# Four sets of seven products for the eight gate blocks of a hybrid decoder layer

## The chip, the cores and the metric

The kernel runs on one core of one Trainium2 chip. A core has TensorE (PE, matrix products; PEld is its weight load), VectorE (DVE), ScalarE (ACT), GpSimd (POOL) and SyncE (SP, which here only issues transfers), an on-chip memory of 128 partitions (SBUF), accumulation banks for TensorE (PSUM) and DMA engines that move data between HBM and SBUF. The engines run side by side and meet at semaphores. The metric is the time of one execution on the device in microseconds; a median of several runs is compared.

## The reference, cut to what matters

A layer for 256 tokens of width 2048. The input is normalised and projected by `w_in`; latent attention (`attn`) and a gated short convolution run beside each other; each result is projected to the width of the model, weighted by a gate from the same input, and the sum is projected once more.

```python
h = _rmsnorm(x, pre_norm_g)
proj = jnp.einsum('bsd,de->bse', h, w_in)
... z_mla, c_in, b_gate, c_gate, z_conv, g_mla, g_conv = jnp.split(proj, cuts, axis=-1)
...
y_mla = jnp.einsum('bse,ed->bsd', attn, w_o_mla)
y_conv = jnp.einsum('bse,ed->bsd', b_gate * conv * jax.nn.silu(z_conv), w_o_conv)
merged = jax.nn.sigmoid(g_mla) * y_mla + jax.nn.sigmoid(g_conv) * y_conv
out = jnp.einsum('bsd,de->bse', merged, w_out)
x = x + _rmsnorm(out, post_norm_g)
```

The change concerns `g_mla`, `g_conv`, `y_mla`, `y_conv` and `merged`: five products of 256x2048 by 2048x2048, the last with `w_out`.

## The kernel before

**Numbers.** Everything is float32, computed by three products of a high and a low part: each weight `raw` is split into `whi` (ScalarE, line 254) and `wlo` (VectorE, line 255), in halves of 128x1024. One weight load ("unit") is 1 MB, four rows of 128 by a column block of 512.

**Blocks.** Each of the five matrices has four column blocks of 512. A plain block is four units of 24 products of 128x512, so 96 products. For the gates there is a cheaper way, `paired` (line 1188): two blocks are taken as a 2x2 problem, the input halves in seven prepared combinations (`form` "11", "5", "6", "7", "22", "3", "12"), the weights in four plain and three summed ones, and seven products take the place of eight. A set has seven items, Q1, V5, V6, V7, V4, V3, Q2, each of two units of 12 products: 168 products for two blocks. The sums are made in SBUF buffers `b` of 8 KB a partition (tags `rt`, `rb`, `rc`, two each): VectorE adds at V5, V6 and V4 (line 1204), and an accumulating DMA of GpSimd adds at V5 what V7 uses (line 1208). V4 loads the `rb` buffers a second time.

**Which blocks.** `paired(c)` takes column c of both gates, c = 1, 2, 3. Column 0 is plain (`gate_block`, line 1109).

**Stages.** A loop over 16 heads (line 902) computes attention and convolution; it keeps x in `x_both`. The forms are made in its first half, stored in HBM (`far_form`) and fetched by `bring_form` (line 1037). Behind the loop the pools of the loop are closed and new ones are laid over them on the right side: `wides` (gates and products, 2 KB each), `sraw` (the sums' buffers) and `forms` (seven times 8 KB). `seq` is a list of units, each with a load, a split, its products and something to do after; the loop at line 1376 issues loads up to four loads ahead and splits two units ahead. Its order: gate block 0 of `g_mla`, of `g_conv`, set 1 with the branch blocks p0 and p1 between its items, set 2 with p2 and most of p3, set 3 with the rest of p3, v0 and v1, then v2 and v3. Here p is `y_mla`, v is `y_conv`, and `at_u`/`cv_u` fetch a quarter of their inputs, turned, into `at_both`/`cv_both`, which take the place of `x_both`. Then comes the output product in the order of `out_order`, and the tail with the last norm and the stores.

**Gates.** A finished gate is written to HBM (`keep`, line 1024) and read again (`again`, line 1030) when its branch block is done: `branch_block` multiplies p by its gate and keeps the product `m`; `merged_block` reads gate and `m`, multiplies and adds, turns the sum and stores it to `far_m` for the output product.

**Queues.** Loads of weights, forms and quarters go out on SP's queue in the order of the program; each waits on SP until its buffer is free. The buffers `raw` (three) are shared by plain units and quarters. Accumulating loads, `m` and `far_m` go out on GpSimd's queue, kept gates on ScalarE's. While the loop runs, `ahead` (line 209) loads three units and splits one unit ahead of the products, past the end of the loop too.

**PSUM.** Plain blocks use four banks `mm`; a set has X (tag `cv`, two), Z (`st`) and Y (`o`).

Of the kernel before, what the change touches and what calls it, by code (L numbers as in the profile page):

```python
# [11 lines left out]
F32 = mybir.dt.float32  # L12
# [70 lines left out]
def tile_layer(ctx: ExitStack, tc: tile.TileContext, xw, w0, xb, x, pos, pvec, post_g, wc, wz, wcv, wkr, wqk, wqr, wv, cwr, wsq, xf, out):  # L83
# [65 lines left out]
    done = {"raw": 0, "split": 0}  # L149

    def load_raw(i):
# [11 lines left out]
        for a, b, piece in pieces:  # L163
            d = nc.sync.dma_start(out=t[:, a:b], in_=piece)
            if i >= u_d[0][0][0]:
                tc.keep_in_program_order(d)
# [6 lines left out]
    def split_unit(i):  # L173
# [22 lines left out]
        for h in range(0, w, HALF):  # L196
            n = min(HALF, w - h)
            if u_out[3, 0] <= i < u_out[3, 3]:
                both = sraw.tile([P, 2, HALF], F32R, name=f"whl{i}_{h}", tag=SRAW[len(last_parts) % 3], bufs=2)
# [9 lines left out]
    def ahead(i, raw=3, split=1):  # L209
        while done["raw"] < min(i + raw, len(plan)):  # L210
            load_raw(done["raw"])
            done["raw"] += 1
        while done["split"] < min(i + 1 + split, len(plan)):
# [79 lines left out]
    xstack = main.enter_context(ExitStack())  # L293
    hp = xstack.enter_context(tc.tile_pool(name="hp", bufs=1))
    x_both = hp.tile([P, KD, 2 * S], F32R, name="x_both")
# [8 lines left out]
    qa = bp.tile([P, KR, 2 * S], F32R, name="qa")  # L304
    ckv = bp.tile([P, KR, 2 * S], F32R, name="ckv")
# [106 lines left out]


# [472 lines left out]

    form_steps = make_forms()
# [14 lines left out]
    for h in range(H):  # L902
        v, at = divmod(h, HV)

        if at == 0:
# [57 lines left out]
        if h < 8:  # L963
            next(form_steps)
            next(form_steps)

# [40 lines left out]
    estack.close()  # L1007
    right = ctx.enter_context(ExitStack())
    wides = right.enter_context(tc.tile_pool(name="wides", bufs=1, side="right", reuse_waits="tile"))
    sraw = right.enter_context(tc.tile_pool(name="sraw", bufs=1, side="right", reuse_waits="tile"))  # L1010
    gstack = ExitStack()
    forms = gstack.enter_context(tc.tile_pool(name="forms", bufs=1, side="right", reuse_waits="tile"))
    SRAW = ("rt", "rb", "rc")
    last_parts = []

    def sum_tile(name, tag):
        return sraw.tile([P, UNIT], F32, name=name, tag=tag, bufs=2)
# [15 lines left out]


    form = {n: forms.tile([P, KH, 2, P], F32R, name=f"form_{n}") for n in FORMS}

    def bring_form(n):
        tc.keep_in_program_order(
            nc.sync.dma_start(
                out=form[n][:, :, :, :].rearrange("p k j c -> p (k j c)").bitcast(F32), in_=far_form[n][:, :]  # L1040
            )
        )
# [66 lines left out]
    def gate_block(c, n, key, afters):  # L1109

        def last(pss):
            for t in range(NT):
                g = wide(f"sg{n}_{c}_{t}", "abcd"[2 * n + t])
                nc.scalar.activation(g[:, :], pss[t][:, :], AF.Sigmoid, scale=r_col[:, t : t + 1])
                keep((key, c, t), g)
            if 3 in afters:
                afters[3]()

        return block(c, n, lambda k: x_both[:, k, :], afters, last)

    def branch_block(c, both):

        y = []

        def early():
            for t in range(NT):
                y.append(wide(f"y{c}_{t}", "y", 2))
                again(("gm", c, t), y[t])

        def last(pss):  # L1130
            if c == 3:
                for t in range(NT):
                    y.append(wide(f"y{c}_{t}", "y", 2))
                    nc.scalar.activation(y[t][:, :], pss[t][:, :], AF.Copy)
                    keep(("y", c, t), y[t])
                return
            early()
            for t in range(NT):
                nc.vector.tensor_tensor(y[t][:, :], pss[t][:, :], y[t][:, :], op=ALU.mult)
                keep(("m", c, t), y[t])  # L1140

        return block(c, 2, lambda k: both[k // 4][:, k % 4, :], {}, last)

    fetches = []

    def merged_block(c, both):

        got = []

        def fetch(t):  # L1150
            g, m = (
                wide(f"v{n}{c}_{t}", "y", 2) if c < 2 else late.tile([P, 512], F32, name=f"v{n}{c}_{t}")
                for n in "gm"
            )
            again(("gc", c, t), g)
            again(("y" if c == 3 else "m", c, t), m)
            q = None
            if c == 3:
                q = late.tile([P, 512], F32, name=f"vq{t}")
                again(("gm", c, t), q)  # L1160
            got.append((g, m, q))

        def soon():
            if c < 2:
                fetch(0)
            elif c == 2:
                for f in fetches[2:]:
                    for t in range(NT):
                        f(t)

        fetches.append(fetch)

        def last(pss):
            for t in range(NT):
                if len(got) <= t:
                    fetch(t)
                g, m, q = got[t]
                if q:
                    nc.vector.tensor_tensor(m[:, :], m[:, :], q[:, :], op=ALU.mult)
# [426 lines left out]
```

## Time and profile before

| | us |
|---|---|
| median of 3 runs | 1052.83 (1050.6 to 1053.73) |
| the profiled execution, its own time | 1049.99 |
| its span, first to last instruction | 1048.2 |
| TensorE busy | 1022.9 |
| VectorE busy | 784.4 |
| ScalarE busy | 580.0 |
| GpSimd busy | 200.3 |

The core's mean granted TensorE clock was 0.99. Lines of the profile name engine, line, operation and the tiles written and read; a table of stretches gives the busy time of each engine with its number of instructions, the granted clock as a share of full speed, the share of time in which the DMA engines were busy, and GB/s. The chain that ended last is followed back from the last instruction, each step to what released it. A wait is put down to the event that came last. Products overlap by their pipeline, so the time of one is read from a run of them, not from its own duration.

### The profile page before, as it was taken

To read this page: it belongs to the slowest core of one execution; us is meant where nothing else is said; L and a number is where in the kernel's file an instruction comes from. 1 tells how busy PE (TensorE), PEld (TensorE's weight loads), DVE (VectorE), ACT (ScalarE), POOL (GpSimd) and SP (SyncE) were. 2 spreads that over 40 slices of the span, in tenths; PEclk is the share of its full clock that TensorE was granted. 3 is DMA by queue.
4 is the path that set the end of the run, shared out by engine and by line. 5 is a ranking of instruction groups with operands and counts; after the bars stand their busy time and mean duration, and the time that the engine had idled before them with its cause. 6 is when DMAs were issued, how large, how long until landed. Compare 5 with 4: busy or idle time off the path is not lost.

```text
span 1048.2 us, 12876 instructions
## 1 busy us (share of the span) xinstructions
PE 1022.9 (98%) x4576; PEld 845.2 (81%) x4576; DVE 784.4 (75%) x1074; ACT 580.0 (55%) x811; POOL 200.3 (19%) x366
## 2 busy tenths in 40 slices
PE   9999999999999999999999999799999999998997
PEld 8888888878788788888888888678888878887886
DVE  7588978779676687777777756778987968666562
ACT  7675646646555555564555545546666655533551
POOL 4620421112411223212233110000100102142000
PEclk9999999999999999999999999899999999999999
DMA  9776778667777676867676799878786785697742
GB/s 355 280 250 227 272 239 284 237 222 285 261 272 256 231 249 223 269 213 231 245 256 210 271 366 359 271 312 327 236 302 247 272 298 181 241 333 306 290 164 81
DMA packets 55153, 273.13 MB, mean 261 GB/s; under 512 B 9232, under 2 KB 11920, under 8 KB 30512
## 3 DMA queue, kind: packets, MB, share of 16 engines
q1 hardware_dynamic: 35280, 213.30, 55.5%
q0 software_dynamic: 16784, 50.98, 15.6%
q10 hardware_dynamic: 3024, 8.01, 1.9%
q8 instruction: 36, 0.59, 0.2%
q14 instruction: 29, 0.24, 0.1%
HBM read 239.78 MB, written 28.31 MB: 256 GB/s over the span
## 4 chain that ended last, share of the span: by engine, by line
PE 72%; DMA 13%; DVE 9%; issue 4%; ACT 2%; POOL 1%; SPq 0%; DVEq 0%; POOLq 0%; ACTq 0%
PE cv L88 28%; PE sq L88 15%; PE out L88 8%; PE z L88 4%; DMA raw<-wsq_dram 3%; DMA b<-wsq_dram 3%; PE qa L88 2%; DMA far_form<-form 2%; PE sX L88 2%; DVE wlo L255 2%; PE ckv L88 2%; PE kn L88 2%; PE qn L88 2%; DVE slo_V L255 1%; DMA cw<-cwr_dram 1%
## 5 line engine op out<-in xcount | busy, mean ns | idle before, releaser
L255 DVE TENSOR_TENSOR wlo<-raw,whi 128x1024 fp32r<-128x1024 f32 (+1 forms) x316 | 371.8, 1192 | 134.8 <-ACT whi L254 128.6
L254 ACT ACTIVATE whi<-raw 128x1024 fp32r<-128x1024 f32 (+1 forms) x318 | 324.1, 1032 | 267.3 <-PE cv L88 98.4
L88 PE MATMUL cv<-whi,x_both 128*128 128x512 f32 x1024 | 321.0, 390 | 3.1 <-DVE vv_lo L255 3.1
L88 PEld LDWEIGHTS cv<-whi,x_both 128*128 128x128 f32 x1024 | 193.0, 188 | 43.7 <-DVE vv_lo L255 3.9
L88 PE MATMUL cv<-wlo,x_both 128*128 128x512 f32 x512 | 200.1, 391 | 0.8 <-DVE wlo L255 0.8
L88 PEld LDWEIGHTS cv<-wlo,x_both 128*128 128x128 f32 x512 | 96.4, 188 | 21.0 <-DVE wlo L255 1.6
L254 ACT ACTIVATE shi_V<-b 128x1024 fp32r<-128x1024 f32 x60 | 61.9, 1057 | 59.7 <-PE sq L88 26.0
L88 PE MATMUL sq<-whi,at_both 128*128 128x512 f32 x256 | 83.3, 398 | 4.4 <-ACT whi L254 4.4
L255 DVE TENSOR_TENSOR slo_V<-b,shi_V 128x1024 fp32r<-128x1024 f32 x60 | 71.2, 1222 | 19.4 <-ACT shi_V L254 19.0
L88 PE MATMUL z<-whi,x_both 128*128 128x512 f32 x256 | 80.0, 389 | 0.0
L88 PE MATMUL sq<-whi,cv_both 128*128 128x512 f32 x256 | 79.8, 389 | 0.0
L340 POOL DMA_DIRECT2D far<-via x64 | 35.4, 559 | 181.1 <-DVE via L332 178.0
L88 PE MATMUL out<-whi,m_both 128*128 128x512 f32 x208 | 65.6, 395 | 0.0
L88 PEld LDWEIGHTS sq<-whi,at_both 128*128 128x128 f32 x256 | 49.5, 193 | 15.4 <-ACT whi L254 5.1
L88 PEld LDWEIGHTS sq<-whi,cv_both 128*128 128x128 f32 x256 | 48.1, 188 | 10.1 <-ACT shi_V L254 0.2
L88 PEld LDWEIGHTS z<-whi,x_both 128*128 128x128 f32 x256 | 48.1, 188 | 9.9
L88 PE MATMUL sq<-wlo,at_both 128*128 128x512 f32 x128 | 51.6, 403 | 2.1 <-DVE wlo L255 2.1
L88 PE MATMUL z<-wlo,x_both 128*128 128x512 f32 x128 | 49.8, 389 | 0.0
L88 PE MATMUL sq<-wlo,cv_both 128*128 128x512 f32 x128 | 49.8, 389 | 0.0
L88 PE MATMUL sX<-shi_V,form 128*128 128x512 f32 x144 | 47.2, 398 | 1.1 <-ACT shi_V L254 1.1
L88 PEld LDWEIGHTS out<-whi,m_both 128*128 128x128 f32 x208 | 39.8, 191 | 8.4
L88 PE MATMUL out<-wlo,m_both 128*128 128x512 f32 x104 | 41.2, 397 | 3.1 <-DVE wlo L255 3.1
(281 smaller groups left out, 1580.0 us busy)
## 6 DMA issues: line engine op xcount, KB each, us to landing
raw<-wcv_dram SPq DMA_DIRECT2D x64, 1024.0 KB, 5.8
raw<-wsq_dram SPq DMA_DIRECT2D x56, 1024.0 KB, 6.6
b<-wsq_dram SPq DMA_DIRECT2D x24, 1024.0 KB, 7.2
raw<-wz_dram SPq DMA_DIRECT2D x16, 1024.0 KB, 5.1
raw<-wqk_dram SPq DMA_DIRECT2D x8, 1024.0 KB, 6.4
far_form<-form POOLq DMA_DIRECT2D x14, 512.0 KB, 7.9
form<-far_form SPq DMA_DIRECT2D x7, 1024.0 KB, 11.6
cw<-cwr_dram POOLq DMA_DIRECT2D x24, 256.0 KB, 6.4
```

Source lines behind the costliest of these rows:

```text
L88: return tc.keep_in_program_order(nc.tensor.matmul(*a, **kw))
L254: a = nc.scalar.activation(hi, src, AF.Copy)
L255: b = nc.vector.tensor_tensor(lo, src, hi.bitcast(F32), op=ALU.subtract)
L340: tc.keep_in_program_order(queue.dma_start(out=f[i], in_=m))
```

## The change

Eight gate blocks become four sets. A set now takes two column blocks of one gate: `g_mla` columns 0 and 1, 2 and 3, then the same of `g_conv`. The plain gate blocks go, and with them `gate_block` and `merged_block`.

A gate stays in its SBUF tile (`gate_of`) and the sums of a branch block stay in their PSUM banks (`sums_of`); whichever comes second calls `weigh` (the product goes to HBM as `m`) or `merge` (the `m` of the same column is fetched ahead through two tiles `y`, added, turned and stored to `far_m`).

`x_both` becomes four tiles, so that quarters of `at` and `cv` replace it one by one. The latents `qa` and `ckv` get a pool of their own (`lp`), which closes at head 14; over it and the early pool a left pool `fleft` holds forms "11", "5" and the sum buffer `rt0`, and the two forms are fetched at heads 14 and 15. Small tiles of the loop are placed first in their pool so that the other sum buffers and forms, now in one pool `spool` in an order written out by hand, lie over tiles that are released early. The merged quarters lie in `spool` over forms 7, 22, 3 and 12.

The loop's `ahead` stops at the loop's last unit. X moves to bank `st`, Z to `cv`. The order of units within the sets is new, and so is the start of `out_order`.

```diff
-    for n, c in [(0, 0), (1, 0)] + [(n, c) for n in (2, 3) for c in range(4)]:
+    for n, c in [(n, c) for n in (2, 3) for c in range(4)]:
...
-    out_order = [(c, k) for c in range(2) for k in range(3)] + [(0, 3), (1, 3)]
+    out_order = [(0, 0), (0, 1), (1, 0), (1, 1), (0, 2), (1, 2), (0, 3), (1, 3)]
...
-        while done["raw"] < min(i + raw, len(plan)):
+        while done["raw"] < min(i + raw, done["end"]):
...
+        if h == H - 2:
+            estack.close()
+            lstack.close()
+            fleft = main.enter_context(tc.tile_pool(name="fleft", bufs=1, reuse_waits="tile"))
+            for n in ("11", "5"):
+                form[n] = fleft.tile([P, KH, 2, P], F32R, name=f"form_{n}", tag=f"f{n}", bufs=1)
...
+        if h >= H - 2:
+            bring_form(("11", "5")[h - (H - 2)])
...
+    sums = {tag: sum_tile(f"first_{tag}", tag) for tag in ("rt0", "rt1", "rb0", "rb1")}
+    for n in ("3", "12"):
+        form[n] = form_tile(spool, n)
+    sums.update({tag: sum_tile(f"first_{tag}", tag) for tag in ("rc0", "rc1")})
+    for n in ("6", "7", "22"):
+        form[n] = form_tile(spool, n)
...
+    def meet(c, t, combine):
+        met[c, t] = met.get((c, t), 0) + 1
+        if met[c, t] == 2:
+            combine(c, t)
...
+    def weigh(nc_, t):
+        n, c = nc_
+        g = gate_of[n, c, t]
+        nc.vector.tensor_tensor(g[:, :], sums_of[n, c][t][:, :], g[:, :], op=ALU.mult)
+        keep(("m", c, t), g)
...
+    def merge(nc_, t):
+        n, c = nc_
+        g, m = gate_of[n, c, t], fetched.pop((c, t))
+        nc.vector.tensor_tensor(g[:, :], sums_of[n, c][t][:, :], g[:, :], op=ALU.mult)
+        nc.vector.tensor_tensor(m[:, :], m[:, :], g[:, :], op=ALU.add)
+        go, _ = turned(m[:, :], g[:, :], 4, far_m[c][:, 512 * t : 512 * (t + 1)])
+        go()
+        fetch()
...
-            tag, bufs = {"X": ("cv", 2), "Z": ("st", 1), "Y": ("o", 1)}[b]
+            tag, bufs = {"X": ("st", 1), "Z": ("cv", 2), "Y": ("o", 1)}[b]
...
+    s0, s1, s2, s3 = (paired(i, *a) for i, a in enumerate(((0, 0, weigh), (0, 2, weigh), (1, 0, merge), (1, 2, merge))))
...
+    interleave(s0, {
+        "Q1": at_u[:1] + p[0][:1] + at_u[1:2] + p[0][1:2] + at_u[2:3] + p[0][2:3], "V5": at_u[3:] + p[0][3:],
+        "V6": p[1][:1], "V7": p[1][1:2], "V4": p[1][2:3], "Q2": p[1][3:],
     })
+    interleave(s1, {"Q1": p[2][:2], "V5": p[2][2:3], "V6": p[2][3:], "V7": p[3][:2], "V3": p[3][2:3], "Q2": p[3][3:]})
     interleave(s2, {
+        "Q1": cv_u[:1] + v[0][:1] + cv_u[1:2] + v[0][1:2], "V5": cv_u[2:3] + v[0][2:3], "V6": cv_u[3:] + v[0][3:],
+        "V7": v[1][:2], "V3": v[1][2:3], "Q2": v[1][3:],
     })
...
     interleave(s3, {
+        "Q1": v[2][:2], "V5": v[2][2:3], "V6": v[2][3:], "V7": v[3][:1], "V3": v[3][1:2],
     })
```

More of the change, by code (lines that the diff above doesn't have):

```diff
@@ L148, in tile_layer @@
     raws, splits, early = {}, {}, {}
-    done = {"raw": 0, "split": 0}
+    done = {"raw": 0, "split": 0, "end": u_d[0][2][0]}
     def load_raw(i):
@@ L1121, in branch_block @@
[L1121 to L1179, printed above, removed]
-                nc.vector.tensor_tensor(g[:, :], pss[t][:, :], g[:, :], op=ALU.mult)
-                nc.vector.tensor_tensor(m[:, :], m[:, :], g[:, :], op=ALU.add)
-                go, _ = turned(m[:, :], g[:, :], 4, far_m[c][:, 512 * t : 512 * (t + 1)])
-                go()
-        return block(c, 3, lambda k: both[k // 4][:, k % 4, :], {1: soon}, last)
@@ L1271, in paired @@
         out = {}
-        for name, (n, k), _, p, f, b, first, last, after in items:
+        for name, (nb, k), _, p, f, b, first, last, after in items:
             us = []
@@ L1374, in tile_layer @@
+    done["end"] = len(plan)
     nl = ns = 0
@@ L1402, in tile_layer @@
     assert not pending
+    assert not wanted and not fetched
     last_m = turned_unit(far_m[3:4], m_b, 3, nc.gpsimd)
```

205 lines of the change are left out of this document (99 added, 106 removed).

## The prediction

> **What bounds the kernel now.** I read the page's first part, then the chain that ended last, then the waits of PE, and last a table of stretches cut where the program's stages end.
>
> ```profile
> span 1048.2 us, 12876 instructions
> PE 1022.9 (98%) x4576; PEld 845.2 (81%) x4576; DVE 784.4 (75%) x1074; ACT 580.0 (55%) x811; POOL 200.3 (19%) x366
> ```
> ```profile
> 599.00 43.58 PE sq L88 x192
> ...
> 713.53 5.44 PE sZ L88 x24
> ...
> 951.18 88.77 PE out L88 x383
> ```
>
> PE is busy for 98% of the span, so its work is the bound; a stage is longer than its matmuls only where PE waits or its clock drops. The price of a matmul is in the chain (start, duration, engine, tile, count): 192 products of the two plain gate blocks took 43.58 us, and 24 of a set of seven 5.44 us. Both give 0.227 us for one of 128x512 (5.44/24 = 0.2267, used below).
>
> The next rows are the stages: the plain gate blocks, the sets for columns 1, 2 and 3 with what runs between, the last two branch blocks, the output product, the tail (busy times of PE, PEld, DVE, ACT, POOL, then granted clock, DMA share, GB/s).
>
> ```profile
> 598.80:642.90 44.10, 44.10 (x197) 36.50 (x196) 24.92 (x27) 19.78 (x22) 4.94 (x9) 1.00 0.94 368
> 642.90:735.30 92.40, 85.80 (x360) 68.97 (x359) 74.49 (x65) 53.48 (x60) 4.05 (x6) 0.96 0.83 302
> 735.30:811.80 76.50, 76.24 (x336) 62.79 (x336) 66.31 (x56) 49.97 (x53) 4.05 (x6) 1.00 0.73 258
> 811.80:904.30 92.50, 90.11 (x387) 73.08 (x386) 77.31 (x73) 55.49 (x61) 12.39 (x21) 0.98 0.75 261
> 904.30:947.80 43.50, 43.50 (x193) 35.87 (x192) 26.07 (x30) 16.41 (x17) 16.66 (x31) 1.00 0.72 260
> 947.80:1040.00 92.20, 89.06 (x387) 73.34 (x386) 50.26 (x54) 38.22 (x51) 4.79 (x9) 0.98 0.59 222
> 1040.00:1048.20 8.20, 1.92 (x8) 1.04 (x6) 3.06 (x6) 2.12 (x6) 0.00 (x0) 0.78 0.35 129
> ```
>
> From the loops in the code these stages hold 360 products (set 1), 336 (set 2), 384 (set 3), 192 and 384 (output). At 0.2267 us that is 81.6, 76.2, 87.1, 43.5 and 87.1 us. The losses are therefore 92.4 - 81.6 = **10.8**, 0.3, 92.5 - 87.1 = **5.4**, 0 and 92.2 - 87.1 = **5.1**: 21.6 us after 599 us. Part is PE waiting, part a low clock after it:
>
> ```profile
> PE sq L88 <- ACT whi L254: 4.4, 1, 4.4
> PE out L88 <- DVE wlo L255: 3.1, 1, 3.1
> ...
> PE sX L88 <- ACT shi_V L254: 1.1, 1, 1.1
> ```
> ```profile
> 681.00:682.00 1.00, 1.00 (x4) 0.50 0.78 197
> ...
> 683.00:684.00 1.00, 1.00 (x6) 1.00 0.99 410
> ...
> 850.00:852.00 2.00, 2.00 (x5) 0.50 0.46 178
> ...
> 952.00:954.00 2.00, 2.00 (x7) 0.60 0.75 164
> ```
>
> In each loss PE stands still (92.40 - 85.80 = 6.6 us in the first, 2.4 and 3.1 in the others), and then runs at clock 0.50 to 0.60 for some microseconds. So a wait costs nearly twice itself (10.8 to 6.6, 5.4 to 2.4). The Trainium skill, TensorE: Matmul & The Clock Gate, "Part 1: The HAM clock gate", says that only an idle window of about 3.4 us puts the clock at half. By that rule the waits of set 3, the longest of which is 1.1 us, would have cost their own 2.4 us and the forecast would be some 2 us lower; the 0.50 at 850 us speaks against it, and the measurement decides.
>
> **What set 1 lost, and why.** SP issues loads in program order, and a load waits for its buffer, with all behind it:
>
> ```profile
> 577.14 22.64 SPq L164 DMA_DIRECT2D raw<-wsq_dram  x5
> ...
> 645.16 0.33 SPq L164 DMA_DIRECT2D raw<-wsq_dram  x1
> ...
> 657.67 0.33 SPq L164 DMA_DIRECT2D raw<-wsq_dram  x1
> ```
> ```profile
> 657.67 16.56 DMA raw<-wsq_dram
> ```
> ```profile
> 630.00:640.00 10.00, 10.00 (x46) 8.29 (x45) 4.90 (x4) 4.37 (x5) 0.00 (x0) 1.00 1.02 428
> ...
> 650.00:660.00 10.00, 10.00 (x46) 8.26 (x45) 10.00 (x10) 4.96 (x6) 1.99 (x3) 1.00 1.01 292
> ...
> 590.00:600.00 10.00, 10.00 (x49) 8.34 (x48) 8.89 (x12) 7.38 (x10) 0.55 (x1) 1.00 0.58 213
> ```
>
> The load of 657.67 landed 16.56 us later, because the DMA engines were full (share 1.01) with a burst that had waited behind the shared raw buffers. PE's 4.4 us wait is that.
>
> **The change, part by part.**
>
> *Fewer products.* A set of seven needs 7 x 24 = 168 products where two plain blocks need 192. Column 0 was plain; now four sets cover all eight gate blocks: 24 products go, 24 x 0.2267 = **-5.44 us**. PE is the bound and nothing replaces them, so this is on the path.
>
> *More VectorE and ScalarE work.*
>
> ```profile
> L255 DVE TENSOR_TENSOR slo_V<-b,shi_V 128x1024 fp32r<-128x1024 f32 x60 | 71.2, 1222 | 19.4 <-ACT shi_V L254 19.0
> L1204 DVE TENSOR_TENSOR b<-b,b 128x2048 f32<-128x2048 f32 x18 | 41.1, 2288 | 4.1 <-DMA b<-wsq_dram 4.1
> L1139 DVE TENSOR_TENSOR y<-sq,y 128x512 f32<-128x512 f32 x6 | 4.0, 688 | 0.0
> L1114 ACT ACTIVATE sg<-sq,r_both 128x512 f32<-128x512 f32 x4 | 2.8, 691 | 3.9 <-PE sq L88 3.9
> ```
> ```profile
> 598.80:605.00 6.20, 6.20 (x30) 5.11 (x28) 6.17 (x11) 3.07 (x5) 1.46 (x3) 1.00 0.68 254
> 800.00:840.00 40.00, 40.00 (x178) 32.83 (x177) 39.97 (x37) 27.61 (x32) 4.04 (x6) 1.00 0.83 292
> ```
>
> A set splits 28 halves at 71.2/60 = 1.19 us on DVE (33.2), adds six pairs of weights at 2.29 (13.7) and three sums at about 0.69 (2.1): 49 us. The plain pair split 16 halves (19.0). DVE gains **30 us**. It had 24.92 + 74.49 + 66.31 + 77.31 + 26.07 = 269 us there, so 299 us beside 1440 x 0.2267 = 326 us of products, 92% against 81%. Hidden as long as splits run ahead; this is the tightest cover of the change. By set, with two blocks each (81.6 us of PE): set 0 has what the first set has now (74.5) plus the tail of head 15, which fills DVE until 605 us (6.17 of 6.20): 80; set 1 has 66.3 and one unit more (2.4): 69; sets 2 and 3, with the merges, about 77. No set exceeds its products. The cost's lower bound is nothing: from 800 to 840 us DVE was busy for 39.97 of 40 us and PE for all 40. Its upper bound is what is lost if DVE gets no more than its share of now (the third rival). I take 1 us in set 0 alone, next to the row of 800 us, which is the nearest. ScalarE gains twelve halves of about 1 us and is busy for 55%: nothing.
>
> *The handover at 599 us.* The plain blocks used weights that the main loop loaded and split ahead. Now the loop stops at its own last load, forms "11" and "5" are fetched at heads 14 and 15 and the sums' buffers are laid over tiles in the order of their release.
>
> ```profile
> 564.13 0.39 PE L88 MATMUL sw<-kr,qr 128*128 128x512 f32 x1
> ```
>
> By the tile sizes, the first three sum buffers in the right pool lie over `kr`, `mask`, `qn`, `kn` and `qr`, last read by these scores of head 15, and the left pool over `qa`/`ckv`, done two heads earlier. SP has only two forms and two sum loads between its last raw load and the gap of 590 us (share 0.58), so both weights of the first item land well ahead of 599 us. The two forms pass no waiting load; 1 MB each is hidden by the three-deep raw loads. Cost 0; if the splits were not drawn forward from behind the loop, PE would wait for one or two units, each 2 x 1.19 us on DVE: 2 to 5 us.
>
> *Gates stay in SBUF.*
>
> ```profile
> vg<-kept_gc POOLq DMA_DIRECT2D x8, 256.0 KB, 5.2
> b<-wsq_dram POOLq DMA_DIRECT2D x6, 1024.0 KB, 12.6
> form<-far_form SPq DMA_DIRECT2D x7, 1024.0 KB, 11.6
> ```
>
> Sixteen gates were written and read back (8 MB); that goes, two accumulating loads of 1 MB come, and the weights stay 8 MB: 6 MB fewer over 326 us, worth nothing by itself. The new wait: a branch bank is held until its gate is there. Of block 0 that is one unit after the last item; the next user of the bank comes 5.44 us later, and sigmoid and product need 0.69 + 0.69. Behind the products, POOL issues the next set's accumulating loads and ACT the copy into the reused gate tile; both have a set's first 16 us. Cost 0, up to 2.
>
> *The order of sets.* Sets 1 to 3 get two plain units ahead of the V5 adds (now one), sets 1 and 2 two behind V7, where the sum buffers are reloaded. Set 3 of now lost its 5.4 us behind the full DVE row of 800 us, with the turned halves of `cv` in it; set 2 inherits those. I give set 2 3 us and sets 1 and 3 2 us together, bounds 0.3 (the best set now) and 5.4 each.
>
> *The first set.* Its burst moves from 645 to about 605 us: four plain loads, two pairs of sums, forms "6" and "7" and two turned halves, some 11 MB, and two accumulating loads, all wanted by PE's 634th us. At the 400 GB/s or so of full rows 11 MB take 28 us of those 29; beside accumulating loads the rate was 292. I take 4 us of PE wait, doubled by the clock to 8; bounds 0.3 (the set at 735 us) and twice the 10.8 of now. The Trainium skill, DMA: Bandwidth & Descriptors, "Where 436 GB/s comes from", puts the HBM limit near 358 GB/s; by it the burst would need 31 us, the wait 3 us more, this term 14 and the forecast 1051. The 428 GB/s at 630 us goes beyond that limit.
>
> *Output and tail* keep their work; the last merge still comes just ahead of them: 5.1 and 8.2 us as now.
>
> **Sum.** Losses 9 (set 0, with DVE's 1) + 3 + 2 + 5.1 = 19.1 against 21.6: -2.5; with -5.4 that is -7.9. The profiled execution took 1049.99 us (1.8 around its span), so 1042.1; the median shown, 1052.83, lies 2.84 above it. Forecast **1044.9 us**.
>
> **The rivals.**
>
> - *Even sets.* Two units of lead and the forms taken out of the burst make every set lose 0.3 as the best one does now: losses 4 x 0.3 + 5.1 = 6.3, -15.3 - 5.4 = -20.7, so 1032. For it: set 2 of now with the same kind of work. Against: fewer plain units to run ahead in. A half-way case is 1038.
> - *The gain is eaten.* Column 0's 43.5 us without a loss were cover in which seven forms and the first sums were fetched; without it set 0 loses 8 us more than forecast, or the handover does not hold: 1053, within 0.3%. Also what a change in name only would give.
> - *VectorE becomes the bound (slower).* In the sets DVE was busy 218.1 of 261.4 us (83%). If dependences keep it from more, 299 us of work need 358 us, where the same stretch now takes 349 and the sum has it near 340: 1053 + 9 = 1062. It decides from 299/349 = 86% downwards. Against: the row of 800 us.
>
> **How the numbers follow.** Forecast and near it (1040 to 1049.6) 0.48; even sets, whole or half, 0.24; eaten 0.15; VectorE, or a first burst as bad, 0.13. A difference of 0.3% (3.2 us) is about what a measurement can tell from none. Faster is 0.72, same 0.15, slower 0.13. The range 1033 to 1055 leaves out most of the slower case and the whole of the evenest one.
>
> **What would show it.** PE's count 4552; a stage of 1440 products after 599 us of 326 us plus its losses; PE's longest wait between 625 and 650 us, ended by a split whose load took over 10 us; no PE wait at 599; DVE near 90% there. Wrong if DVE is full and PE waits in all sets, if PE waits at the handover, or if the set's losses vanish.

## The result, and the profile after

The changed kernel is slower. Its median is 1066.92 us against 1051.71 us, four runs each; the ratio is 1.014 with a 95% interval of 1.0097 to 1.0183. The forecast was 1044.9 us, 0.7% faster; the sign was wrong. One execution of e5_pool_add, described below, ran at a granted clock of 0.56 and took 1708.69 us; it is in no ratio, and as it is the profiled one, e5 has no row in the table of stages. The first lines of the page of the changed kernel show the span and the busy time of each engine:

```profile
span 1067.4 us, 12811 instructions
PE 1022.0 (96%) x4552; PEld 843.2 (79%) x4552; DVE 812.6 (76%) x1095; ACT 590.9 (55%) x824; POOL 192.9 (18%) x354
```

The 24 products are gone (4552 matmuls instead of 4576), yet the span is 19.2 us longer (the medians differ by 15.2; the profiled execution was the slowest of the four). A table of stretches of the changed kernel, cut where the loop's last product ends and then at the first product of each further set, of the output and of the tail (busy times of PE, PEld, DVE, ACT, POOL, then granted clock, DMA share, GB/s), shows where the time went:

```profile
599.90:709.20 109.30, 89.55 (x361) 71.25 (x361) 84.07 (x78) 57.37 (x65) 7.32 (x12) 0.89 0.78 292
709.20:791.10 81.90, 81.90 (x362) 67.50 (x361) 70.93 (x63) 52.01 (x55) 4.68 (x8) 1.00 0.66 226
791.10:880.05 88.95, 83.42 (x361) 68.64 (x360) 72.91 (x63) 51.98 (x55) 6.58 (x11) 0.96 0.77 268
880.05:966.85 86.80, 83.81 (x361) 68.56 (x360) 77.45 (x74) 51.75 (x55) 16.65 (x29) 0.98 0.60 199
966.85:1059.65 92.80, 89.21 (x385) 73.16 (x384) 46.86 (x51) 36.83 (x48) 5.49 (x10) 0.98 0.59 214
1059.65:1067.40 7.75, 2.16 (x9) 1.24 (x7) 3.06 (x6) 2.15 (x6) 0.00 (x0) 0.94 0.37 135
```

A set with its two branch blocks holds 360 products, 81.6 us. Set 1 takes 81.9, so the price of a product and the gain from 24 fewer are right. Set 0 takes 109.3: a loss of 27.7 us where 9 was forecast. Set 2 loses 7.4 (forecast 3), set 3 5.2 (2 for sets 1 and 3 together), the output 5.7 (5.1). Of the 27.1 us by which the span misses its forecast (1042.1 less 1.8, so 1040.3), set 0 makes 18.7.

The waits of PE between 590 and 690 us (in total, times, longest) name two places in it:

```profile
PE sX L88 <- DVE slo_V L255: 9.9, 3, 8.7
PE sX L88 <- DVE slo_Q L255: 4.9, 1, 4.9
PE sX L88 <- ACT shi_Q L254: 2.5, 1, 2.5
```

**The first place is the handover.** ScalarE's timeline, then VectorE's, with the idle time before an instruction in brackets:

```profile
600.59 0.69 ACT L799 ACTIVATE cg<-cv,r_both 128x512 f32<-128x512 f32 x1 [4.18 <-DVE cv_w L801]
...
601.44 3.89 ACT L254 ACTIVATE shi_Q<-first_rt 128x1024 fp32r<-128x1024 f32 x4
```
```profile
606.36 0.71 DVE L347 STREAM_TRANSPOSE mv<-cv_f 128x512 f32<-128x512 f32 x1
606.99 4.59 DVE L255 TENSOR_TENSOR slo_Q<-first_rt,shi_Q 128x1024 fp32r<-128x1024 f32 x4
```

The weights of Q1 had landed, but their splits stood on both engines behind the loop's tail: on ScalarE behind `cg`, on VectorE behind the last transposition. TensorE had nothing else to do. Its clock fell with it:

```profile
605.00:610.00 5.00, 1.77 (x4) 1.49 (x5) 4.97 (x7) 2.31 (x4) 3.95 (x8) 0.50 0.54 174
```

PE reached the first plain unit at 615.76 us by the chain of waits. From 599.90, with 5.44 us of Q1's own products, that is 10.4 us late.

**The second place follows from the first.** SP's timeline, and four rows of the chain that ended last:

```profile
589.02 0.33 SPq L1129 DMA_DIRECT2D turned<-far_at  x1
612.82 0.33 SPq L164 DMA_DIRECT2D raw<-wsq_dram  x1
...
616.67 0.90 SPq L1196 DMA_DIRECT2D first_rb<-wsq_dram  x2
```

```profile
621.09 1.21 DVE at_both L255 x2
622.32 0.33 SPq L164
...
623.80 26.02 DMA first_rc<-wsq_dram
...
649.92 2.29 DVE first_rt L1204
```

The table of stretches for this part:

```profile
600.00:612.80 12.80, 5.43 (x13) 3.98 (x13) 11.95 (x18) 8.75 (x12) 4.91 (x9) 0.60 0.27 82
612.80:636.00 23.20, 22.53 (x98) 17.94 (x96) 18.25 (x17) 12.28 (x16) 1.84 (x2) 1.00 0.93 356
636.00:650.00 14.00, 8.45 (x36) 6.68 (x36) 5.84 (x6) 2.30 (x3) 0.00 (x0) 0.88 1.01 287
```

The three `raw` buffers held a plain unit and two turned quarters. Their splits stood behind Q1's on ScalarE and VectorE; the first quarter's ended on VectorE at 612.79. So SP issued nothing from 589 to 612.8 us, 23.4 of them waiting for that split, and the DMA engines ran at a share of 0.27 just when there was room (last table, first row). Then everything came at once. The chain shows the same link once more: the splits that ended at 622.30 freed a buffer, SP's load into it went out at 622.32, and only behind it the second load of `rc`, at 623.80. That load took 26.02 us to land, VectorE's sum waited for it, and PE's 8.7 us wait ended at 653.4. The last row shows a full DMA share with only 287 GB/s: at 629.9 and 632.4 us the two accumulating loads had joined. The transfers of the changed kernel from 629.9 to 650 us, by queue (packets, MB, share of 16 engines; q1 holds SP's loads, q0 GpSimd's):

```profile
q1 hardware_dynamic: 573, 4.17, 51.6%
q0 software_dynamic: 288, 2.10, 50.5%
```

Half of the engines' time went to each, but half as many bytes to the accumulating ones: 0.516 x 20.1 / 4.17 = 2.5 us of all 16 engines per MB of plain load, 0.505 x 20.1 / 2.10 = **4.8 us** per MB of accumulating load.

### The profile page after: what moved, and what is told of

It is laid out like the page before. It is cut to its first block, busy times and chain, and to the rows that moved or that the text cites. A ratio compares the mean times of both kernels' runs of the same rounds, so it can differ in the third digit from the quotient of the medians.

```text
span 1067.4 us, 12811 instructions
## 1 busy us (share of the span) xinstructions
PE 1022.0 (96%) x4552; PEld 843.2 (79%) x4552; DVE 812.6 (76%) x1095; ACT 590.9 (55%) x824; POOL 192.9 (18%) x354
## 4 chain that ended last, share of the span: by engine, by line
PE 66%; DMA 16%; DVE 10%; issue 3%; ACT 2%; POOL 2%; SPq 0%; DVEq 0%; POOLq 0%; ACTq 0%
PE cv L88 24%; PE sq L88 10%; PE out L88 7%; PE sX L88 7%; DMA b<-wsq_dram 4%; PE z L88 4%; PE sZ L88 3%; DMA cw<-cwr_dram 3%; DMA first_rc<-wsq_dram 2%; DVE wlo L255 2%; PE qa L88 2%; PE ckv L88 2%; DMA far_form<-form 2%; PE qn L88 1%; PE sY L88 1%
## 5 line engine op out<-in xcount | busy, mean ns | idle before, releaser
L255 DVE TENSOR_TENSOR wlo<-raw,whi 128x1024 fp32r<-128x1024 f32 (+1 forms) x300 | 352.0, 1187 | 100.8 <-ACT whi L254 95.6
L254 ACT ACTIVATE whi<-raw 128x1024 fp32r<-128x1024 f32 (+1 forms) x302 | 306.7, 1029 | 218.6 <-PE cv L88 90.0
L88 PE MATMUL sq<-whi,at_both 128*128 128x512 f32 x256 | 81.0, 390 | 0.0
L88 PE MATMUL sX<-shi_V,form 128*128 128x512 f32 x192 | 64.7, 408 | 1.7 <-ACT shi_V L254 1.7
L88 PE MATMUL sX<-slo_V,form 128*128 128x512 f32 x96 | 39.9, 415 | 11.7 <-DVE slo_V L255 11.7
```

The costliest lines, as they stand in the source:

```text
L88: return tc.keep_in_program_order(nc.tensor.matmul(*a, **kw))
L254: a = nc.scalar.activation(hi, src, AF.Copy)
L255: b = nc.vector.tensor_tensor(lo, src, hi.bitcast(F32), op=ALU.subtract)
```

## The experiments

Two theories stood after this. **A:** the order of the work at a set's start, in which loads are asked for late and then collide with accumulating loads. **B:** VectorE, at 305 us in four sets of 367, is too full. The expectations name a third, **C:** the accumulating loads fill the DMA engines. From e10 on, each expectation gives the letters A and B anew. All ratios below are to the kernel before on the same chip. Stages are cut by PE's timeline as above and come from one execution each, ratios from all.

| kernel | ratio (95%) | set 0 | set 1 | set 2 | set 3 | output |
|---|---|---|---|---|---|---|
| the change | 1.014 (1.0097 to 1.0183) | 109.3 | 81.9 | 89.0 | 86.8 | 92.8 |
| e1_split_ahead | 1.0151 (1.011 to 1.0192) | 105.0 | 81.9 | 90.4 | 85.4 | 89.4 |
| e2_sums_first | 1.0081 (1.0056 to 1.0106) | 96.5 | 81.9 | 89.0 | 87.0 | 91.9 |
| e3_small_adds | 1.0014 (0.9983 to 1.0045) | 102.6 | 81.6 | 83.4 | 81.6 | 89.8 |
| e4_small_accum | 0.9961 (0.9939 to 0.9983) | 94.7 | 81.9 | 81.6 | 83.0 | 89.7 |
| e6_dve_add | 1.0113 (1.0065 to 1.016) | 100.1 | 85.7 | 83.6 | 85.5 | 88.7 |
| e8_pool_first_ahead | 1.0231 (1.0183 to 1.028) | 100.3 | 88.7 | 89.6 | 91.1 | 92.5 |
| e9_dve_first_ahead | 1.0054 (1.0025 to 1.0083) | 96.5 | 85.7 | 84.7 | 85.9 | 94.0 |
| e11_mix | 0.9979 (0.9954 to 1.0005) | 94.1 | 81.9 | 85.0 | 85.0 | 93.5 |
| e12_sums_later | 0.9989 (0.9968 to 1.001) | 94.4 | 81.9 | 87.8 | 84.9 | 92.0 |
| e13_handover_alone | 1.001 (0.9985 to 1.0035) | 99.4 | 81.9 | 81.8 | 85.3 | 92.4 |
| e14_order_and_sums | 0.9963 (0.994 to 0.9986) | 94.5 | 81.9 | 83.5 | 85.0 | 89.6 |
| e15_pinned | 1.0016 (0.9988 to 1.0044) | 100.9 | 81.9 | 81.8 | 85.1 | 91.0 |

One execution can mislead. The one shown was 7.8 us below its kernel's median for e6, 7.3 for e3 and 5.7 for e4; the others were within 3. The output has the same work in every row and took 88.7 to 94.0 us.

### One edit each: split, order, sums, accumulating loads

**e1_split_ahead** loads and splits Q1's two units by the loop's own `ahead`. They then come twice, once through `raw` for Q1 and once into `rt` for the sum of V5, 2 MB more.

```diff
+    u_q1 = [add(wsq[0, 0, k]) for k in range(2)]
...
+                if i == 0 and name[:2] == "Q1":
+                    u = u_q1[src[1]]
+                    if done["split"] <= u:
+                        split_unit(u)
+                        done["split"] += 1
+                    return pieces(splits.pop(u))
```

> The changed kernel, with the two weights of item Q1 of set 0 loaded and split by the head loop's own running ahead (a second copy of 2 x 1 MB through the raw buffers), as the plain gate blocks were before. Theory A (handover and transfer order): in the changed kernel PE waited 2.5 and 4.9 us at 600 us because these splits stand behind the loop's tail on ScalarE and VectorE, and ran at a low clock until 612 us, 10.1 us in all; with the splits ahead that wait falls to 0 to 3 us and the time by 5 to 10 us, to about 1057 to 1062 us. Theory B (VectorE has too much to do): the same work is only moved, so the microseconds come back later in set 0 and the time stays within 3 us of 1067.

PE's waits of this kernel between 590 and 690 us:

```profile
PE sX L88 <- DVE slo_V L256: 6.6, 3, 5.5
PE sq L88 <- ACT whi L255: 4.5, 1, 4.5
```

Q1's waits of 7.4 us are gone, but the unit behind it now waits 4.5 us for the same engines, and the `rc` wait is still 5.5. Set 0 gains 4.3 us; the time doesn't move. Drawing one item forward moved the wait to the next.

**e2_sums_first** asks for the loads of set 0's sums ahead of the plain loads.

```diff
+    sums_load = [s0[nm][u][0] for nm in ("V5", "V6") for u in range(2)]
...
+    at1_load = at_u[1][0]
+    at_u[1][0] = lambda: (at1_load(), [ld() for ld in sums_load])
```

> The changed kernel, with only the order of SP's queue changed in set 0: the loads of the sum buffers rb and rc go out right behind the second quarter, ahead of the plain loads that wait for raw buffers. Theory A: PE's wait of 8.7 us at 645 us, which ended with a load of rc that landed 26 us after its issue, goes (below 2 us), and with its low clock 8 to 13 us, so 1054 to 1059 us. Theory B: VectorE has the same work in the same places, so the wait is replaced by others and the time stays within 3 us of 1067. Theory C (the accumulating loads fill the DMA engines): the wait shrinks to about half.

The 8.7 us wait is gone and set 0 is 12.8 us shorter; the handover stays. Its two waits in this kernel:

```profile
PE sX L88 <- DVE slo_Q L255: 4.9, 1, 4.9
...
PE sX L88 <- ACT shi_Q L254: 2.3, 1, 2.3
```

Only the order differs, with no byte and no instruction less. The ratio is 0.6% lower, but the two intervals overlap; the wait that is gone is the firmer evidence. It is the first for A.

**e3_small_adds** cuts VectorE's additions to 64 of 2048 columns, so the sums of V5, V6 and V4 are incomplete.

```diff
-                    nc.vector.tensor_tensor(t[:, :], t[:, :], raw[plus][:, :], op=ALU.add)
+                    nc.vector.tensor_tensor(t[:, :64], t[:, :64], raw[plus][:, :64], op=ALU.add)
```

> The changed kernel, with the adds of weights on VectorE (V5, V6, V4) done on 64 of 2048 columns, so that the sums are incomplete; every wait stays, and VectorE does about 24 x 2.2 = 53 us less. Theory B: the waits of PE in sets 0, 2 and 3 go, 15 to 35 us, so 1032 to 1052 us. Theory A: the loads still land late; only the 2.2 us of an add behind a late load and the half of the clock go, 4 to 10 us, so 1057 to 1063 us.

**e4_small_accum** cuts the accumulating loads to 64 of 2048 columns, so V7's sums are incomplete.

```diff
-    nc.gpsimd.dma_start(out=raw[1, k][:, :], in_=wsq[n, c + 1, 2 + k], accum_op=ALU.add)
+    nc.gpsimd.dma_start(out=raw[1, k][:, :64], in_=wsq[n, c + 1, 2 + k][:, :64], accum_op=ALU.add)
```

> The changed kernel, with the accumulating loads at V5 cut to 64 of 2048 columns, so that V7's sums are incomplete; their order and waits stay. Theory C: the loads of rc land 8 to 13 us earlier in sets 0 and 2, and the time falls by 10 to 20 us, to 1047 to 1057 us. Theory A: the burst behind the raw buffers remains, the time falls by 3 to 8 us, to 1059 to 1064 us. Theory B: within 3 us of 1067.

The same view as above of e4_small_accum, for sets 0 and 2, and of e3_small_adds for set 3:

```profile
598.20:692.90 94.70, 85.24 (x362) 68.69 (x362) 84.02 (x78) 56.88 (x65) 7.34 (x12) 0.95 0.80 316
...
774.80:856.40 81.60, 81.60 (x362) 67.59 (x361) 73.10 (x63) 52.00 (x55) 6.51 (x11) 1.00 0.72 269
```
```profile
863.50:945.10 81.60, 81.60 (x362) 67.57 (x361) 66.42 (x71) 52.40 (x55) 16.69 (x29) 1.00 0.63 210
```

Without the accumulating loads' bytes set 0 loses 13.1 us, most of it at the handover, whose waits of 2.5 and 4.9 us are still there, and set 2 nothing, with VectorE as busy as before (73.10 against 72.91). Cutting VectorE's additions cures set 3 (VectorE 66.42 instead of 77.45) and helps set 2, but set 0 keeps 21.0 of its 27.7. So in these executions the accumulating loads' bytes make 14.6 us of set 0 and 7.4 of set 2; VectorE's fill matters in set 3, which took 83.0 us in e4.

The shares can't be added. By its median, 1051.9 us, e3 lies inside B's range, and e4, at 1044.3, below C's. Each takes back nearly all of the 1.4%, and e13 below does so with neither cut. Late loads, accumulating loads and long additions cost this much only together in these runs.

### The sums V7 by another engine

**e5_pool_add** and **e6_dve_add** make V7's sums on GpSimd and on VectorE; e8_pool_first_ahead and e9_dve_first_ahead do the same with the edits of e1 and with the sums' loads ahead as in e2.

```diff
-                if name[:2] == "V5":
+                if name[:2] == "V6":
                     k = plus[1]
...
-                        nc.gpsimd.dma_start(out=raw[1, k][:, :], in_=wsq[n, c + 1, 2 + k], accum_op=ALU.add)
+                        nc.gpsimd.tensor_tensor(raw[1, k - 2][:, :], raw[1, k - 2][:, :], raw[1, k][:, :], op=ALU.add)
```
```diff
-                if plus and name[:2] != "V7":
+                if plus:
                     nc.vector.tensor_tensor(t[:, :], t[:, :], raw[plus][:, :], op=ALU.add)
-                if name[:2] == "V5":
...
```

> The changed kernel, complete, with V7's sums made by an add of 128x2048 on GpSimd (behind V6's, from the rc buffer that is there anyway) in place of the accumulating loads. Theory C (an accumulating load of 1 MB holds the DMA engines about twice as long as a plain one, and that is what starves sets 0, 2 and 3): set 0 near 95 us, set 2 near 82, as with the small accumulating loads, and a ratio to the kernel before of 0.99 to 1.00. Theory B (VectorE is the bound): set times as in the changed kernel (109, 89, 87), ratio 1.01 to 1.02. If GpSimd's add is slow beside VectorE, V7 waits for it and the ratio lies between.

> The changed kernel, complete, with V7's sums made by VectorE at V7 in place of the accumulating loads: 8 x 2.3 = 18 us more on VectorE, 8 MB less on the DMA engines. Theory B: slower than the changed kernel, ratio 1.02 to 1.035. Theory C: sets 0 and 2 become shorter by 10 and 5 us in spite of VectorE's work, ratio 0.995 to 1.005.

> The changed kernel, complete, with GpSimd's add for V7, set 0's sums loaded ahead of the plain loads, and Q1's splits ahead in the loop. If the three causes (accumulating loads, the place of the sums in SP's order, the handover) are the whole of the loss, set 0 falls from 109 to 84 to 90 us, set 2 and 3 to about 82, and the ratio to 0.98 to 0.99. If VectorE (B) is behind part of it, set 0 stays above 93 us.

> As the kernel before it, but with V7's add on VectorE, which has 18 us more to do (97% of the sets' products instead of 92%). Theory B: 1 to 2% above the one with GpSimd's add. Theory C and a fast enough VectorE: within 0.5% of it, ratio 0.98 to 0.995.

e5 came out at 1.0221 (1.0173 to 1.0269), e8 no better, both above all that was expected: GpSimd is the wrong place. Two groups of e8_pool_first_ahead, and the first one again in the changed kernel, both from 600 to 950 us (busy us, mean ns):

```profile
L256 DVE TENSOR_TENSOR wlo<-raw,whi 128x1024 fp32r<-128x1024 f32 x60 | 91.7, 1556 | 6.8 <-ACT whi L255 5.8
...
L1215 POOL TENSOR_TENSOR b<-b,b 128x2048 f32<-128x2048 f32 x6 | 37.3, 6227 | 9.1 <-DMA b<-wsq_dram 9.1
```
```profile
L255 DVE TENSOR_TENSOR wlo<-raw,whi 128x1024 fp32r<-128x1024 f32 x60 | 71.3, 1218 | 6.1 <-ACT whi L254 5.0
```

The addition takes 6227 ns there (a rough figure, as GpSimd's spans in the profile are), and VectorE's own split beside it 1556 ns instead of 1218. In e9, which has the sums on VectorE and the other edits of e8, on the same chip, the split's mean is 1218 ns again. The Trainium skill, GPSIMD Engine Reference, "3.1 Elementwise — side-by-side cycle accounting", gives 4497 ns for GpSimd's addition of this length and 2293 for VectorE's; the second agrees with the 2285 ns here, the first does not. Its "1. Specifications" says that GpSimd shares its SBUF interfaces with VectorE, with contention when an instruction of VectorE has two inputs in SBUF; the slower splits agree.

On VectorE a sum takes those 2285 ns, but VectorE is too full. The stretch of set 1 of e6_dve_add:

```profile
697.35:783.05 85.70, 83.52 (x361) 68.65 (x360) 75.22 (x65) 51.99 (x55) 2.84 (x6) 0.98 0.50 191
```

Two additions more (75.22 us of VectorE instead of 70.93) bring 3.8 us of loss to the one set that had none; PE's only wait there, 2.2 us, ends with a split of VectorE. Sets 0 and 2 became shorter all the same, as C had it, but the ratio, 1.0113, did not follow, and e9 came to 1.0054 where C expected 0.98 to 0.995. So theory B holds as a limit to what VectorE can take over; that it is not the whole of the loss rests on e13 below.

### Did the kernel before pay as well?

**e10_before_small_accum** makes e4's cut in the kernel before.

> The kernel before with its six accumulating loads cut to 64 of 2048 columns; the sums V7 are then incomplete, the products and splits are all still there. The same cut in the changed kernel (eight such loads) took its ratio from 1.014 to 0.996, 0.018 or 19 us. Theory A (the accumulating loads hold the DMA engines at stages' starts whatever the order, and the kernel before pays for its six as well): ratio to the kernel before of 0.982 to 0.991, 9 to 19 us gained, most of it out of set 1 and set 3, where it lost 10.8 and 5.4 us. Theory B (they cost only where the changed order puts them, in bursts of two sets of seven products; the kernel before hides its own): 0.996 to 1.002. If A holds, two accumulating loads more are only a part of what the change lost, and the rest is the first set's handover.

The ratio was 0.9898 (0.9849 to 0.9947). Two stretches, its set 1 and the one from its set 3 to the output:

```profile
643.40:730.90 87.50, 84.45 (x362) 68.49 (x362) 74.74 (x65) 53.56 (x60) 4.05 (x6) 0.98 0.78 299
...
807.60:938.30 130.70, 130.70 (x577) 107.95 (x576) 103.41 (x102) 71.81 (x78) 28.93 (x52) 1.00 0.70 256
```

Set 1 took 92.4 in the kernel before, and the second stretch 92.5 + 43.5 = 136.0. About 10 us of the 21.6 that the kernel before lost were its six accumulating loads. The change has eight.

### Order and sums together

**e11_mix** takes Q1 and the quarters at0 and at1 into the loop, makes V7 by VectorE in set 0, by accumulating loads in set 1, one of each in sets 2 and 3, and asks early for the sums' loads in sets 0 and 2.

```diff
+                by_dma = plus and plus[1] % 2 < (0, 2, 1, 1)[i]
+                if plus and not (name[:2] == "V7" and by_dma):
...
+        if h == H - 1:
+            quarter_split(0)
+            quarter_load(1)
...
+    cv1_load = cv_u[1][0]
+    cv_u[1][0] = lambda: (cv1_load(), [ld() for ld in rc_load])
```

> The changed kernel with three edits, nothing left out: the first set's Q1 units and two quarters are loaded and split in the last stage of the loop; the sums V7 are made by VectorE in set 0, by accumulating loads in set 1, by one of each in sets 2 and 3; the two loads of a sum go ahead of the plain loads in sets 0 and 2. Theory A (the loss is the accumulating loads, where VectorE is too full to make all the sums, and the handover at the loop's end): four of eight accumulating loads and no handover wait should take set 0 from 109 to about 90 us and set 2 from 89 to about 84: about 1067-19-5 = 1043, ratio 0.99 (0.985 to 1.000). Theory B (VectorE is the bound as soon as it makes any sum): set 0 stays above 97 us or set 1 goes above 85, ratio 1.003 to 1.010, as in the run where it made all of them.

At 0.9979 it is level with the kernel before. One row of its ScalarE timeline shows what set 0 still lost at the handover:

```profile
605.46 0.60 ACT L1262 ACTIVATE sa<-sX 128x512 f32<-128x512 f32 x1 [6.17 <-DVE mv L348]
```

The copy of Q1's bank stood ahead of the next splits, and it waited for VectorE's tail since the gates' tiles are laid over the loop's.

**e12_sums_later** mends that (the copy comes two units later and the splits ahead of it are pinned) and asks for set 0's loads in the order of their use. **e13_handover_alone** is e12 with all eight accumulating loads back.

```diff
-            ("Q1", (0, 0), "rt", None, "11", "X", True, False, lambda: copy("a", "X")),
+            ("Q1", (0, 0), "rt", None, "11", "X", True, False, lambda: later(2, lambda: copy("a", "X"))),
...
+    p[0][1][0] = lambda: (p00_load(), [ld() for ld in sums_load[:4]])
+    p02_load = p[0][2][0]
+    p[0][2][0] = lambda: (p02_load(), [ld() for ld in sums_load[4:]])
```
```diff
-                by_dma = plus and plus[1] % 2 < (0, 2, 1, 1)[i]
+                by_dma = plus and plus[1] % 2 < 2
```

> The kernel e11_mix (ratio 0.9979) with its order at the loop's end changed, nothing left out: the plain product's first two units are loaded ahead of the units of the first sum, those of the later sums behind its third, and ScalarE copies the bank of Q1 behind the splits of two more units (in e11_mix it stood ahead of them and waited 6.2 us for VectorE's last transposition). Theory A (what is left of set 0's loss, 12.5 us, is the order of loads and copies at the handover): set 0 from 94 to 85 to 89 us, ratio 0.989 to 0.994. Theory B (it is the volume, 14 MB in 34 us at 415 GB/s, so any order loses it somewhere): set 0 stays at 92 to 96 us, ratio 0.996 to 1.000.

> The kernel e12_sums_later with all eight accumulating loads put back, so the changed kernel with the handover's order alone mended, nothing left out. Theory A (handover and accumulating loads are two separate losses, some 13 and 14 us in set 0): set 0 loses the accumulating loads' share alone and takes 93 to 98 us, set 2 stays at 88 to 90, ratio 1.000 to 1.007. Theory B (the loads that hold the engines are the one cause, and an order only moves the wait, as when Q1's split ahead moved it to the first plain unit): set 0 stays above 101 us, ratio 1.009 to 1.015.

e12 left set 0 where it was: 94.4 us, as its theory B said. e13 is the telling run. With every accumulating load in it, 2 MB more of plain loads and VectorE as busy as in the change (812.2 us in the span, 812.6 there), order alone brings the change from 1.014 to 1.001, and its set 2, forecast at 88 to 90, loses nothing. Its set 0, at 99.4 us, lies between its two theories and is no shorter than with e2's single edit (96.5). Against e12, which differs only in who makes four of the V7 sums, set 0 is 5.0 us longer and set 2 6.0 shorter. Its row for the stretch in which SP had stood still, and those of its sets 0 and 2:

```profile
600.00:612.80 12.80, 9.26 (x41) 7.32 (x40) 11.91 (x17) 5.14 (x6) 4.92 (x9) 1.00 1.01 405
```
```profile
598.90:698.25 99.35, 86.98 (x362) 69.60 (x362) 79.58 (x72) 52.11 (x58) 7.33 (x12) 0.95 0.90 343
...
780.10:861.95 81.85, 81.85 (x362) 67.50 (x361) 73.76 (x63) 51.88 (x55) 6.60 (x11) 1.00 0.77 269
```

The DMA engines are full in the 12.8 us in which they idled before (405 GB/s instead of 82). In set 2 the reason is plain in the queues. The changed kernel's SP row and its row in the chain, then the two accumulating loads in GpSimd's timeline:

```profile
796.98 1.46 SPq L1196 DMA_DIRECT2D b<-wsq_dram  x2
```
```profile
796.98 16.85 DMA b<-wsq_dram
```
```profile
795.23 0.89 POOL L1208 DMA_DIRECT2D b<-wsq_dram  x1
799.33 0.88 POOL L1208 DMA_DIRECT2D b<-wsq_dram  x1 [3.21 <-DVE b L1204]
```

and SP's row for the same loads in e13_handover_alone, with its first accumulating load behind it:

```profile
772.04 1.24 SPq L1217 DMA_DIRECT2D b<-wsq_dram  x2
```
```profile
784.67 0.89 POOL L1236 DMA_DIRECT2D b<-wsq_dram  x1 [1.92 <-ACT whi L255]
```

In the change the loads of `rc`, needed next, went out between the two accumulating ones and took 16.85 us to land. They stood on SP behind a load into `raw` that waited 11.3 us for its buffer, until a split of VectorE was done: the same link as in set 0. In e13 they went out 12.6 us before the first accumulating load. Either edit, no accumulating loads (e4) or early operands (e13), takes set 2 to within 0.3 us of its products. So in set 2 the 4.8 us per MB cost something only where a load that was needed soon stood beside them.

**e14_order_and_sums** has VectorE make set 0's sums, accumulating loads the others', with `rc` early in set 3 too. **e15_pinned** pins set 0's additions and splits to the order of their products.

```diff
-                by_dma = plus and plus[1] % 2 < (0, 2, 1, 1)[i]
+                by_dma = plus and plus[1] % 2 < (0, 2, 2, 2)[i]
...
+    v20_load = v[2][0][0]
+    v[2][0][0] = lambda: (v20_load(), [ld() for ld in rc3_load])
```
```diff
+                    if i == 0:
+                        tc.keep_in_program_order(add)
...
-                    split_act(hi[:, :], lo[:, :], t[:, h * HALF : (h + 1) * HALF])
+                    split_act(hi[:, :], lo[:, :], t[:, h * HALF : (h + 1) * HALF], i == 0)
```

> The mended order at the loop's end, set 0's sums V7 by VectorE, those of sets 1 to 3 by accumulating loads whose other operand is loaded ahead of plain loads (in set 3 now as well as in set 2); nothing left out. Theory A (an accumulating load costs nothing where its operands are asked for early: with that order set 2 took 81.8 us with both its accumulating loads, where the change took 89.0): sets 1 and 2 at 82, set 3 at 82 to 84 instead of 85 to 87, set 0 at 94 as before; about 598 + 94 + 82 + 82 + 83 + 92 and some 10 of end = 1041, ratio 0.992 to 0.996. Theory B (the accumulating loads hold the DMA engines twice as long wherever they stand, so earlier ones only move the wait): set 2 or set 3 stays at 85 to 89 or the output part grows by as much, ratio 0.998 to 1.003.

> The kernel e14_order_and_sums with set 0's additions and splits pinned to the order in which their products come (in the run before VectorE made the sums V7 ahead of the splits of V5 and TensorE waited 3.6 us for one of these); nothing left out. Theory A (order again): set 0 from 94 to 90 to 92 us, ratio 0.002 to 0.004 below that of e14_order_and_sums. Theory B (the volume of loads in the first 40 us decides, an addition out of its place only fills time that is lost anyway): set 0 stays at 93 to 95, same ratio within 0.002.

e14 is faster than both kernels: 0.9963 (0.994 to 0.9986) of the kernel before, so about 0.9963 / 1.014 = 0.983 of the change, from runs on two chips. Its gain is a little below what was expected, for set 3 did not move (85.0 us). There VectorE has the merges too, 77.0 of 85.0 us by the same view; e3, with short additions, is the one run whose set 3 took 81.6. Its set 2 took 83.5 us, where e13 and e15 with the same order there took 81.8. Set 0 still loses 12.9 us. A 10 us row of e14 in it, a row of its chain, two of VectorE and one of PE:

```profile
620.00:630.00 10.00, 7.40 (x24) 5.76 (x25) 8.54 (x8) 7.06 (x8) 0.00 (x0) 0.83 1.02 428
```
```profile
612.15 14.62 DMA turned<-far_at
```
```profile
606.77 0.71 DVE L348 STREAM_TRANSPOSE mv<-cv_f 128x512 f32<-128x512 f32 x1
607.40 4.59 DVE L256 TENSOR_TENSOR wlo<-raw,whi 128x1024 fp32r<-128x1024 f32 x4
```
```profile
608.64 0.50 PE L88 MATMUL sq<-wlo,at_both 128*128 128x512 f32 x1 [3.38 <-DVE wlo L256]
```

The DMA engines are full, at 428 GB/s, and a quarter's load of 0.5 MB takes 14.62 us to land, which speaks for volume. But PE's longest wait in the set, 3.4 us, is the handover once more: VectorE's splits stand behind its last transposition. How the 12.9 us divide between the two is not shown. e15 speaks against one other order of VectorE: set 0 got 6.4 us longer. Its VectorE timeline:

```profile
606.18 4.59 DVE L256 TENSOR_TENSOR wlo<-raw,whi 128x1024 fp32r<-128x1024 f32 x4
617.62 1.29 DVE L256 TENSOR_TENSOR at_both<-turned,at_both 128x512 fp32r<-128x512 f32 x2 [6.85 <-ACT at_both L255]
```

Pinned to the order of the products, VectorE idles for 6.85 us behind a late quarter; free, it made additions in that time. Neither of e15's theories had it slower. A set 0 with fewer bytes in its first 40 us, without Q1's weights loaded twice, was not tried.

## Why the prediction was wrong

**Fewer products, -5.44 us: right.** Set 1 shows it, and the count.

**The handover, cost 0: wrong, 10.4 us.** The step argued from loads alone: "both weights of the first item land well ahead of 599 us". They did. The condition that it named, splits not drawn forward from behind the loop, is what happened, and its price of 2 to 5 us was too low for three reasons. Two engines stood in turn (2.5 us, then 4.9), the clock fell to 0.50 behind them, and the next units' splits stood in the same queue. The row to see it was in the prediction: VectorE busy for 6.17 of 6.20 us up to 605. It was counted as work of VectorE, not as the time before which no split of set 0 can start. The prediction's own sign of being wrong, a wait of PE at the handover, came.

**The first set's burst, 8 us: mis-sized, about 17 (27.7 less 10.4).** The mechanism was right: the longest wait, 8.7 us, ended at 653 by a split whose load took 26.02 us. Two inputs were wrong. The burst did not move "to about 605 us" but to 612.8, since SP stood at buffers whose splits were late. And the two accumulating loads got no time of their own beside the 28 us of the 11 MB. The prediction had seen the 292 GB/s beside such loads and held it for a slow stretch, not for a price: 4.8 against 2.5 us per MB.

**Gates in SBUF, "6 MB fewer, worth nothing by itself": half right.** The 6 MB brought nothing that a run shows. The two accumulating loads in that sum were not nothing: without the bytes of all eight the change falls from 1.014 to 0.996, and the kernel before, with six, from 1 to 0.990.

**Sets 1 to 3, 5 us: 12.9.** Set 1 as the best set of before (0.3). Set 2 was given its loss for VectorE's row at 800 us; it was `rc` between accumulating loads, late behind a buffer that SP waited 11.3 us for. Set 3 is in the main VectorE with the merges, as e3 shows; but e4, with VectorE's work unchanged, had 83.0 us there, so the accumulating loads have a part in it.

**VectorE, 299 us: 305.** The cover held in set 1 (70.93 us in 81.90, no wait), so the third rival, VectorE as the bound everywhere, did not come. It does limit the cure: sums on VectorE cost set 1 3.8 us.

**The rivals.** What came is the cause of the second, cover lost and a handover that does not hold, at a size beyond the third's 1062 us. The second was priced at 8 us more than the forecast; set 0, with the two failed steps, is 18.7 us over. "A first burst as bad" had a share of the 0.13 for slower. A large part of the error was one missed link: a late split holds a buffer, the buffer holds SP, and the DMA engines idle before the burst. In e2, where the sums' loads pass the held buffers, set 0 is 12.8 us shorter.

**The clock.** The Trainium skill, TensorE: Matmul & The Clock Gate, "Part 1: The HAM clock gate", asks for some 3.4 us of idle time before half clock. Here the row of 605 us (0.50 beside the waits of 2.5 and 4.9 us) agrees with it; the 0.50 after waits of at most 1.1 us in the kernel before did not.

## What to carry to other kernels

Where a stage is moved up to a loop's end, look for the engines' last instructions of that loop, not only for the loads: a split that stands behind them starts no earlier, and the buffer that it holds stops the queue that fills it. Price an accumulating transfer by the DMA time it takes, twice a plain load's here, and ask for the loads that are needed next well ahead of it. When a wait goes by drawing one item forward, look at the next item before you count the gain.

## What the runs showed of the hardware

An accumulating load took 4.8 us of all 16 DMA engines per MB, a plain one 2.5, in the same stretch. GpSimd's addition of two 128x2048 tiles took 6.2 us where VectorE needs 2.3, and VectorE's splits of plain units in the same sets took 1556 instead of 1218 ns. A full row of plain loads moved 428 GB/s (e14).
